# The second half of an out-projection by pairs of token tiles, with seven block products in place of eight for six of its eight k-tiles

## The chip, the cores and the metric

The kernel runs on one core of a Trainium2 chip. The time is device microseconds of one execution; a version is told by the median of its runs. PE is TensorE's matmul, PEld its weight load, DVE is VectorE, ACT is ScalarE, POOL is GpSimd and SP is SyncE, which issues nearly all DMA transfers. The chain of work, the durations and the waits come from a hardware trace of one profiled execution.

## The reference, cut to what matters

One layer: RMSNorm, an in-projection, a bidirectional state-space mixer with a gate, an out-projection with a residual add, and a final RMSNorm. There are 1024 tokens, `d_model` is 1024 and the mixer's inner width 2048. The change concerns the last four lines.

```python
u = rmsnorm(h, norm_w[i])
# ssd_mixer: in-projection, conv, scan in two directions, then
y = y.reshape(b, l, D_INNER) * jax.nn.silu(z.astype(jnp.float32))
yg = y.reshape(b, l, SSD_GROUPS, D_INNER // SSD_GROUPS)
yg = yg * lax.rsqrt(jnp.mean(yg * yg, axis=-1, keepdims=True) + EPS)
y = (yg.reshape(b, l, D_INNER) * norm_w.astype(jnp.float32)).astype(u.dtype)
out = y @ w_out                       # (1024, 2048) @ (2048, 1024)
h = h + out
return rmsnorm(h, final_norm_w)
```

## The kernel before

**Precision.** Each float32 operand of a large product is split into a high part (a cast to `fp32r`) and a low part (the rest, by a subtraction), and a product is three matmuls: high by high, high by low, low by high. In the names `yh` and `yl`, `wo..h` and `wo..l` are such pairs.

**Stages.** After RMSNorm, in-projection and convolution, eight groups of channels go through the scan (`ssd_units`), whose results `yt` are written to `y_d` in HBM, transposed. The out-projection takes the 2048 inner channels as 16 k-tiles of 128 rows, in two halves of 8. In the first half (`half` 0, weights `wo1`) `out_unit(0, t)` handles one tile of 128 tokens: 8 k-tiles by 3 passes by 2 column halves of 512, which is 48 matmuls into one accumulator `po` (128x1024 in PSUM). VectorE adds `po` to the residual `h` (line 565), and SyncE stores the sum in `h_d` (line 566). Units 0 to 3 stand between steps of the last scan group, units 4 to 7 behind it. The second half (`half` 1, weights `wo2`, loaded and scaled by `load_wo` two rows after each of the units 4 to 7) does the same from `h_d`, and then the final norm: add (line 571), square with a row sum on ScalarE (line 572), the root by `rstd_of` (lines 82 and 85), the scaling (lines 580 to 587) and the store to `out`. The last unit cuts its columns into 512, 256 and 256, in accumulators of their own, so that its adds and squares can begin early.

**Names.** In the profile and in the order, a name such as `h05` is the residual tile of half 0, token tile 5; `yt06` is the loaded slice of `y_d` for half 0, token tile 6, and `po10` the accumulator of half 1, tile 0.

**What sets the order.** `out_prep` issues the load of the next unit's `yt` (line 532) and `h` (line 534), and its cast (537) and subtraction (538), in the middle of a unit's matmuls. Every engine and the queue of SyncE work strictly in the order of the built program, and a DMA that must wait for a buffer or for a result holds what stands behind it in that queue. The order is fixed by a list scheduler when the program is built. Buffers are rooms of a pool, by tag: a new tile of a tag waits until the one that had its room is read. `yt` uses the tag `th` (2 rooms), the raw weight rows the tag `raw` (2 rooms), `h` the tag `xc` (3 rooms), `yh` and `yl` the tags `wh` and `wl` (4 rooms each).

Of the kernel before, what the change touches and what calls it, by code (L numbers as in the profile page):

```python
# [31 lines left out]
def kernel(  # L32
# [508 lines left out]
    def out_unit(half, t, wo, prep, nxt):  # L541
        h, yh, yl = prep
        tok = slice(t * P, (t + 1) * P)
        last = half == 1 and t == NC - 1
        cols = [slice(0, 512), slice(512, 1024)]
        ka = [(k, a) for k in range(NO) for a in range(3)]
        if last:

            cols[1:] = [slice(512, 768), slice(768, 1024)]
            steps = [(k, a, i) for i in range(3) for k, a in ka]  # L550
            pos = [pst(f"po{i}")[:, 0:cs.stop - cs.start] for i, cs in enumerate(cols)]
        else:
            po = ps_ip.tile([P, DM], F32, tag="ip", name=f"po{half}{t}")
            pos = [po[:, cs] for cs in cols]
            steps = [(k, a, i) for k, a in ka for i in range(2)]
        nprep = None
        for j, (k, a, i) in enumerate(steps):
            if j == len(steps) // 2 and nxt is not None:
                nprep = out_prep(*nxt)
            l_ = (yh, yh, yl)[a][:, k, :]  # L560
            r_ = wo[k][(0, 1, 0)[a]]
            nc.tensor.matmul(pos[i], l_, r_[:, cols[i]],  # L562
                             start=k == 0 and a == 0, stop=k == NO - 1 and a == 2)
        if half == 0:
            nc.vector.tensor_tensor(out=h, in0=po, in1=h, op=ALU.add)
            nc.sync.dma_start(out=h_d[tok, :], in_=h)
            return nprep
# [1 line left out]
        ss = ops.tile([P, 3], F32, tag="ss", name=f"oss{t}")
        for i, (cs, pi) in enumerate(parts):  # L570
            nc.vector.tensor_tensor(out=h[:, cs], in0=pi, in1=h[:, cs], op=ALU.add)  # L571
            nc.scalar.activation(out=pi, in_=h[:, cs], func=AF.Square, accum_out=ss[:, i:i + 1])
            if last:
                nc.vector.tensor_tensor(out=h[:, cs], in0=h[:, cs], in1=fnw[:, cs], op=ALU.mult)
# [75 lines left out]
```

## Time and profile before

| | before |
|---|---|
| median of 3 runs | 985.52 us (984.31 to 987.09) |
| the profiled execution's own time | 985.42 us |
| its span, first to last instruction | 983.7 us |
| PE busy | 945.5 us (96%), 5220 matmuls |
| VectorE busy | 727.9 us (74%) |
| ScalarE busy | 539.2 us (55%) |
| chain that ended last | PE 56%, VectorE 12%, DMA 12%, ScalarE 12% |

The span is that of the traced instructions; the execution's own time has 1.7 us around it. Busy shares are means over all stages. The chain that ended last is followed back from the last instruction, at each step to what released it; its shares say where a saved microsecond would show.

### The profile page before, as it was taken

What the parts mean: (1) busy time and instruction counts of PE and PEld (TensorE: products, weight loads), DVE (VectorE), ACT (ScalarE), POOL (GpSimd) and SP (SyncE); (2) the same over time, 40 slices, a digit from 0 to 9 for tenths busy, and PEclk for the clock granted to TensorE, in tenths of its full rate; (3) what the DMA queues carried; (4) which work ended last, traced back from release to release, by engine and by line L of the source; (5) the groups of instructions that cost most, each with busy time, mean ns of one, the idle gap of its engine ahead of it and who ended that gap; (6) DMA issues with size and microseconds to landing.
All of it is one profiled execution on the core that took longest, in us unless ns stands there. A gap on an engine that the chain in (4) does not pass through costs nothing.

```text
span 983.7 us, 15133 instructions
## 1 busy us (share of the span) xinstructions
PE 945.5 (96%) x5220; PEld 806.1 (82%) x5220; DVE 727.9 (74%) x1552; ACT 539.2 (55%) x1458; POOL 53.8 (5%) x88
## 2 busy tenths in 40 slices
...
GB/s 223 95 86 97 43 70 94 111 70 70 101 120 53 74 99 124 49 75 98 126 52 82 86 129 63 78 80 126 96 64 142 172 264 174 200 278 142 118 85 65
DMA packets 157325, 107.62 MB, mean 109 GB/s; under 512 B 75248, under 2 KB 133312, under 8 KB 157248
## 3 DMA queue, kind: packets, MB, share of 16 engines
...
## 4 chain that ended last, share of the span: by engine, by line
PE 56%; DVE 12%; DMA 12%; ACT 12%; issue 6%; POOL 2%; SPq 1%; DVEq 0%; POOLq 0%; ACTq 0%
PE po L562 16%; PE ipx L180 12%; PE ipC L180 9%; DMA fb<-rows_d 7%; PE ipB L180 7%; ACT yo L479 3%; DVE x L196 3%; ACT fb L424 2%; PE pz L157 2%; PE pyo L462 2%; PE pyd L468 2%; PE sb L393 2%; ACT fb L419 2%; DVE mt L429 1%; PE sf L393 1%
## 5 line engine op out<-in xcount | busy, mean ns | idle before, releaser
L479 ACT ACTIVATE yo<-pyo,ecs 128x64 f32<-128x64 f32 x448 | 103.1, 320 | 35.8 <-PE pyo L462 30.2
L419 ACT ACTIVATE fb<-fb,cfb 128x128 f32<-128x128 f32 x256 | 85.1, 399 | 55.1 <-DMA fb<-rows_d 49.6
L424 ACT ACTIVATE fb<-fb,cfb 128x128 f32<-128x128 f32 x256 | 84.0, 398 | 3.8 <-DVE fb L421 3.7
L196 DVE SCALAR_TENSOR_TENSOR x<-ipx,prm,x 128x1022 f32<-128x1022 f32 (+1 forms) x64 | 81.1, 1268 | 3.7 <-ACT x L190 3.6
L157 PE MATMUL pz<-wz_1l,uh 128*128 128x256 f32 (+1 forms) x248 | 73.0, 294 | 2.0 <-DVE wz_1l L123 2.0
L157 PE MATMUL pz<-wz_0h,ul 128*128 128x256 f32 (+1 forms) x248 | 73.3, 296 | 0.4 <-DVE ul L301 0.2
L157 PE MATMUL pz<-wz_0l,uh 128*128 128x256 f32 (+1 forms) x248 | 72.0, 290 | 0.0
L157 PE MATMUL pz<-wz_0h,uh 128*128 128x256 f32 (+1 forms) x248 | 71.2, 287 | 0.0
L157 PE MATMUL pz<-wz_1h,ul 128*128 128x256 f32 (+1 forms) x248 | 70.9, 286 | 0.0
L468 PEld LDWEIGHTS pyd<-xb,mt 128*128 128x128 f32 x512 | 66.7, 191 | 4.9 <-DVE mt L429 1.8
L157 PE MATMUL pz<-wz_1h,uh 128*128 128x256 f32 (+1 forms) x248 | 70.4, 284 | 0.0
L471 DVE SCALAR_TENSOR_TENSOR y<-xb,coef,pyd 128x64 f32<-128x64 f32 x256 | 62.5, 273 | 10.5 <-PE pyd L468 10.3
L468 PE MATMUL pyd<-xb,mt 128*128 128x64 f32 x512 | 64.7, 269 | 0.0
L429 DVE TENSOR_TENSOR mt<-fb,pcb 128x512 f32<-128x512 f32 x64 | 43.1, 681 | 15.3 <-PE pcb L427 13.0
L385 DVE TENSOR_TENSOR pb<-pb,sb 128x256 f32<-128x256 f32 x48 | 19.8, 412 | 42.0 <-PE sb L393 41.1
L421 DVE COPY_PREDICATED fb<-trif,fb 128x512 f32<-128x512 uint32 x64 | 47.1, 736 | 3.7 <-ACT fb L419 3.6
L157 PEld LDWEIGHTS pz<-wz_1l,uh 128*128 128x128 f32 x248 | 46.9, 189 | 3.4 <-DVE wz_1l L123 3.2
L157 PEld LDWEIGHTS pz<-wz_0h,ul 128*128 128x128 f32 x248 | 47.2, 190 | 1.3 <-DVE ul L301 1.1
L571 DVE TENSOR_TENSOR h<-po,h 128x1024 f32<-128x1024 f32 (+2 forms) x10 | 10.1, 1011 | 51.3 <-PE po L562 51.3
L157 PEld LDWEIGHTS pz<-wz_0h,uh 128*128 128x128 f32 x248 | 47.1, 190 | 0.5
L157 PEld LDWEIGHTS pz<-wz_0l,uh 128*128 128x128 f32 x248 | 47.1, 190 | 0.0
L157 PEld LDWEIGHTS pz<-wz_1h,ul 128*128 128x128 f32 x248 | 46.9, 189 | 0.2
...
## 6 DMA issues: line engine op xcount, KB each, us to landing
fb<-rows_d SPq DMA_DIRECT2D x128, 256.0 KB, 4.3
y_d<-yt SPq DMA_DIRECT2D x256, 32.0 KB, 2.0
wo<-in_ssd_w_out_dram SPq DMA_DIRECT2D x16, 512.0 KB, 4.2
yt<-y_d SPq DMA_DIRECT2D x16, 512.0 KB, 5.1
xt<-in_x_dram SPq DMA_DIRECT2D x8, 512.0 KB, 5.9
h<-in_x_dram SPq DMA_DIRECT2D x8, 512.0 KB, 4.8
h_d<-h SPq DMA_DIRECT2D x8, 512.0 KB, 3.0
h<-h_d SPq DMA_DIRECT2D x8, 512.0 KB, 3.6
```

Of the source, the lines that this page charges most:

```text
L157: nc.tensor.matmul(pz[:, i, 0:m], a[:, k, tok], b, start=at == 0, stop=at == 3 * NK - 1)
L180: nc.tensor.matmul(ps[:, half * 512:(half + 1) * 512], a[:, k, :], b[:, k, :], start=n == 0, stop=n == 3 * NK - 1)
L196: nc.vector.scalar_tensor_tensor(out=acc[:, o], in0=ps[:, i], scalar=w(k), in1=acc[:, o], op0=ALU.mult, op1=ALU.add)
L393: nc.tensor.matmul(ps[:, 0:CW], xb[:, CW:CW + P], xw, start=True, stop=True)
L419: nc.scalar.activation(out=ef[:, h], in_=ef[:, h], func=AF.Identity, bias=cfb[:, 1, c, hsl(g, h)])
L421: nc.vector.copy_predicated(ef, trif.bitcast(U32).unsqueeze(1).broadcast_to([P, HG, P]), fb[:, 0])
L424: nc.scalar.activation(out=ef[:, h], in_=ef[:, h], func=AF.Exp, bias=cfb[:, 0, c, hsl(g, h)])
L429: nc.vector.tensor_tensor(out=mt, in0=ef, in1=pcb[:, 0:P].unsqueeze(1).broadcast_to([P, HG, P]), op=ALU.mult)
L468: nc.tensor.matmul(pyd[:, cs], mt[:, h, :], xb[:, cs], start=True, stop=True)
L471: nc.vector.scalar_tensor_tensor(out=y[:, cs], in0=xb[:, cs], scalar=coef[:, h:h + 1], in1=pyd[:, cs], op0=ALU.mult, op1=ALU.add)
L479: nc.scalar.activation(out=yo[:, cs], in_=pyo[:, d * CW + h * HD:d * CW + (h + 1) * HD], func=AF.Copy, scale=ecs[:, d, c, hsl(g, h)])
L562: nc.tensor.matmul(pos[i], l_, r_[:, cols[i]], start=k == 0 and a == 0, stop=k == NO - 1 and a == 2)
```

## The change

The 2048 x 1024 product of the second half is rearranged for pairs of token tiles. For six of its eight k-tiles, taken as two groups of three (`HK`), two token tiles of a pair, the two groups and the two column halves make a 2 by 2 by 2 block product. It is computed with seven block products in place of eight, from sums and differences of the blocks:

- Weight operands: `w11`, `w21` (blocks themselves), `t1`, `t2`, `t3` (differences of blocks), made by `weights_a(k)` from two loaded and scaled rows, for k = 0, 1, 2 ahead of units 4, 5 and 6 of the first half; `w22` = `t2` + `t1` and `t4` = `w21` - `t2`, made on chip from the split parts of the others by `weights_b` behind unit 7.
- Token operands per pair: `a11`, `a12`, `a22` and `s1` to `s4`, made by `pair_prep` from two loaded `yt` tiles.
- The two k-tiles left over stay an ordinary product: weights `wd` (`weights_d`, ahead of unit 7) and token operand `e`, in four parts (`plain`) of 6 matmuls for a pair.

A block product is 9 matmuls (3 k-tiles by 3 passes) of 128 tokens by 512 columns. The results are shared among the four blocks of the output by accumulating in PSUM and by copies from one accumulator to another on ScalarE (lines 713, 721 and 732); one product (`pw`, named `p50` to `p53` in the program) is added to two blocks by VectorE (line 717). These line numbers are the changed kernel's. There `out_unit` has its matmuls in line 552, its add in 554 and its store in 555, `out_prep` loads in 533 and 535 and splits in 538 and 539; `split` casts in 589 and subtracts in 590, `scaled_row` loads in 594 and scales in 595; products are line 687, adds 696 with the square in 697. The five decay tables and `trif` move from the pool `const` to a pool `dec` that is closed after the scan.

```diff
--- before.py
+++ after.py
...
+    dec = main.enter_context(tc.tile_pool(name="dec", bufs=1))
+    cfb = dec.tile([P, 2, NC, NH], F32, name="cfb")
...
-        last = half == 1 and t == NC - 1
...
+        for k in range(NO):
...
+            for a in range(3):
+                for cs in (slice(0, 512), slice(512, 1024)):
+                    nc.tensor.matmul(po[:, cs], (yh, yh, yl)[a][:, k, :], wo[k][(0, 1, 0)[a]][:, cs],
+                                     start=k == 0 and a == 0, stop=k == NO - 1 and a == 2)
...
-        parts = list(zip(cols, pos)) if last else [(slice(0, DM), po)]
...
+        nc.vector.tensor_tensor(out=h, in0=po, in1=h, op=ALU.add)
+        nc.sync.dma_start(out=h_d[tok, :], in_=h)
...
+    HK = 3
+    LO, HI = slice(0, 512), slice(512, 1024)
+    def operand(pool, tag, name):
+        t_ = pool.tile([P, 2, HK, 512], R32, tag=tag, name=name)
+        return t_[:, 0], t_[:, 1]
+    def split(src, dst):
+        nc.scalar.copy(dst[0], src)
+        nc.vector.tensor_tensor(out=dst[1], in0=src, in1=dst[0].bitcast(F32), op=ALU.subtract)
+    def scaled_row(n):
+        raw = wp.tile([P, DM], F32, tag="raw", name=f"wa{n}", bufs=2)
+        nc.sync.dma_start(out=raw, in_=w_out[:, NO + n, :])
+        nc.scalar.activation(out=raw, in_=raw, func=AF.Copy,
+                             scale=prm[:, 192 + NO + n:193 + NO + n])
+        return raw
+    def minus(out, a, b):
+        nc.vector.tensor_tensor(out=out, in0=a, in1=b, op=ALU.subtract)
+    W = {n: operand(op2, "o" + n, "o" + n) for n in ("w11", "t1", "t2", "w21", "t3")}
+    wd = op2.tile([P, 2, 2, DM], R32, name="wd")
+    def weights_a(k):
+        ra, rb = scaled_row(k), scaled_row(k + HK)
+        r11, r12, r21, r22 = (r[:, cs] for r in (ra, rb) for cs in (LO, HI))
+        d3 = cp.tile([P, 512], F32, tag="th", name=f"da{k}")
+        split(r11, [p_[:, k] for p_ in W["w11"]])
+        minus(d3, r22, r12)
+        minus(r12, r12, r11)
+        split(r12, [p_[:, k] for p_ in W["t1"]])
+        minus(r22, r22, r12)
+        split(r22, [p_[:, k] for p_ in W["t2"]])
+        split(r21, [p_[:, k] for p_ in W["w21"]])
+        split(d3, [p_[:, k] for p_ in W["t3"]])
+    def weights_d():
+        for j in range(2):
+            split(scaled_row(2 * HK + j), [wd[:, p_, j] for p_ in range(2)])
+    def weights_b(n, a, b, op, tag):
+        W[n] = operand(up, tag, "o" + n)
+        for k in range(HK):
+            d = wp.tile([P, 2, 512], F32, tag="raw", name=f"d{n}{k}", bufs=2)
+            for p_ in range(2):
+                nc.vector.tensor_tensor(out=d[:, p_], in0=W[a][p_][:, k].bitcast(F32),
+                                        in1=W[b][p_][:, k].bitcast(F32), op=op)
+            nc.vector.tensor_tensor(out=d[:, 0], in0=d[:, 0], in1=d[:, 1], op=ALU.add)
+            split(d[:, 0], [p_[:, k] for p_ in W[n]])
+    def pair_prep(i):
+        ys, hs = [], []
+        for t in (2 * i, 2 * i + 1):
+            yt = cp.tile([P, NO, P], F32, tag="th", name=f"yt1{t}")
+            nc.sync.dma_start(out=yt, in_=y_v[:, NO:2 * NO, t * P:(t + 1) * P])
+            ys.append([yt[:, q].rearrange("p k t -> p (k t)")
+                       for q in (slice(0, HK), slice(HK, 2 * HK), slice(2 * HK, NO))])
+        for t in (2 * i, 2 * i + 1):
+            h = cp.tile([P, DM], F32, tag="xc", name=f"h1{t}", bufs=3)
+            nc.sync.dma_start(out=h, in_=h_d[t * P:(t + 1) * P, :])
+            hs.append(h)
+        (a11, a12, e1), (a21, a22, e2) = ys
+        A = {}
+        rooms = {}
+        N = HK * P
+        def put(n, *srcs):
+            at = len(A)
+            if at % 2 == 0:
+                rooms["h"] = wp.tile([P, 2, 512], R32, tag="wh", name=f"yh{i}_{n}", bufs=4)
+                rooms["l"] = wp.tile([P, 2, 512], R32, tag="wl", name=f"yl{i}_{n}", bufs=4)
+            m = len(srcs) * srcs[0].shape[1]
+            room = [rooms[p_][:, at % 2, 0:m] for p_ in "hl"]
+            for j, src in enumerate(srcs):
+                c = slice(j * m // len(srcs), (j + 1) * m // len(srcs))
+                split(src, [r[:, c] for r in room])
+            A[n] = [r.rearrange("p (k t) -> p k t", t=P) for r in room]
+        def room(n):
+            t_ = wp.tile([P, 2, 512], F32, tag="raw", name=f"s{n}_{i}", bufs=2)
+            return t_[:, 0, 0:N], t_[:, 1, 0:N]
+        put("a11", a11)
+        s1, s2 = room("a")
+        nc.vector.tensor_tensor(out=s1, in0=a21, in1=a22, op=ALU.add)
+        put("s1", s1)
+        minus(s2, s1, a11)
+        put("s2", s2)
+        put("a12", a12)
+        put("e", e1, e2)
+        s3, s4 = room("b")
+        minus(s3, a11, a21)
+        put("s3", s3)
+        minus(s4, a12, s2)
+        put("s4", s4)
+        put("a22", a22)
+        return A, hs
+    def product(ps, a, w, fresh, cs=LO, end=True):
+        n, last = 0, 3 * a[0].shape[1] - 1
+        for k in range(a[0].shape[1]):
+            for l_, r_ in ((a[0], w[0]), (a[0], w[1]), (a[1], w[0])):
+                nc.tensor.matmul(ps, l_[:, k, :], r_[:, k, cs], start=fresh and n == 0,
+                                 stop=end and n == last, skip_group_check=True)
+                n += 1
+    def plain(ps, A, j, cs, end):
+        product(ps, [p_[:, 2 * j:2 * j + 2] for p_ in A["e"]], (wd[:, 0], wd[:, 1]), False, cs, end)
+    def add(h, cs, ps, ss, i):
+        nc.vector.tensor_tensor(out=h[:, cs], in0=ps, in1=h[:, cs], op=ALU.add)
+        nc.scalar.activation(out=ps, in_=h[:, cs], func=AF.Square, accum_out=ss[:, i:i + 1])
+        if i:
+            nc.vector.tensor_tensor(out=ss[:, 0:1], in0=ss[:, 0:1], in1=ss[:, i:i + 1], op=ALU.add)
+    def finish(t, h, ss):
+        r = rstd_of(ops, ss[:, 0:1], DM, EPS, f"o{t}")
+        nc.vector.scalar_tensor_tensor(out=h, in0=h, scalar=r, in1=fnw, op0=ALU.mult, op1=ALU.mult)
+        nc.sync.dma_start(out=out[t * P:(t + 1) * P, :], in_=h)
+    def pair_unit(i, prep, nxt):
+        A, (h1, h2) = prep
+        t1, t2 = 2 * i, 2 * i + 1
+        ss1, ss2 = (ops.tile([P, 3], F32, tag="ss", name=f"oss{i}_{j}") for j in range(2))
+        c1 = ps_ip.tile([P, DM], F32, tag="ip", name=f"po1{i}")
+        c11, c12 = c1[:, LO], c1[:, HI]
+        product(c12, A["a11"], W["w11"], True)
+        nc.scalar.copy(c11, c12)
+        pw = pst(f"p5{i}")
+        product(pw, A["s1"], W["t1"], True)
+        for h in (h1, h2):
+            nc.vector.tensor_tensor(out=h[:, HI], in0=pw, in1=h[:, HI], op=ALU.add)
+        product(c12, A["s2"], W["t2"], False)
+        c2 = ps_ip.tile([P, DM], F32, tag="ip", name=f"po2{i}")
+        c21, c22 = c2[:, LO], c2[:, HI]
+        nc.scalar.copy(c22, c12)
+        product(c11, A["a12"], W["w21"], False, end=False)
+        plain(c11, A, 0, LO, True)
+        nprep = pair_prep(nxt) if nxt is not None else None
+        add(h1, LO, c11, ss1, 0)
+        if nxt is None:
+            plain(c12, A, 0, HI, False)
+            product(c12, A["s4"], W["w22"], False)
+            add(h1, HI, c12, ss1, 1)
+            finish(t1, h1, ss1)
+        product(c22, A["s3"], W["t3"], False)
+        nc.scalar.copy(c21, c22)
+        plain(c22, A, 1, HI, True)
+        add(h2, HI, c22, ss2, 0)
+        if nxt is not None:
+            plain(c12, A, 0, HI, False)
+            plain(c21, A, 1, LO, False)
+            product(c12, A["s4"], W["w22"], False)
+            add(h1, HI, c12, ss1, 1)
+            product(c21, A["a22"], W["t4"], False)
+            finish(t1, h1, ss1)
+            add(h2, LO, c21, ss2, 1)
+            finish(t2, h2, ss2)
+            return nprep
+        nc.vector.tensor_tensor(out=h2[:, HI], in0=h2[:, HI], in1=fnw[:, HI], op=ALU.mult)
+        for j, cs in enumerate((slice(0, 256), slice(256, 512))):
+            plain(c21[:, cs], A, 1, cs, False)
+            product(c21[:, cs], A["a22"], W["t4"], False, cs)
+        for j, cs in enumerate((slice(0, 256), slice(256, 512))):
+            add(h2, cs, c21[:, cs], ss2, 1 + j)
+            nc.vector.tensor_tensor(out=h2[:, cs], in0=h2[:, cs], in1=fnw[:, cs], op=ALU.mult)
...
     fnw = op2.tile([P, DM], F32, name="fnw")
+    for t in range(NC // 2, NC):
+        if t < NC - 1:
+            weights_a(t - NC // 2)
+        else:
+            weights_d()
+            pre0 = pair_prep(0)
+        prep = out_unit(0, t, wo1, prep, (0, t + 1) if t < NC - 1 else None)
     nc.sync.dma_start(out=fnw, in_=final_norm_w.rearrange("(o d) -> o d", o=1).partition_broadcast(P))
-    wo2 = []
...
-    for t in range(NC):
-        prep = out_unit(1, t, wo2, prep, (1, t + 1) if t < NC - 1 else None)
+    weights_b("w22", "t2", "t1", ALU.add, "uh0")
+    weights_b("t4", "w21", "t2", ALU.subtract, "ul0")
+    prep = pre0
+    for i in range(NC // 2):
+        prep = pair_unit(i, prep, i + 1 if i + 1 < NC // 2 else None)
```

The order of the built program is shown at three places. The first is the queue of SyncE around the store of `h05`, in the first half's unit 5. Before, the loads of `yt06` and `yt07` stand here:

```order
L532 DMA yt06_9348<-y_d_81 128x8x128
L496 DMA y_d_81<-yt7_5_9083 32x8x32 x4
L566 DMA h_d_8163<-h03_8925 128x1024
L532 DMA yt07_9415<-y_d_81 128x8x128
L532 DMA yt10_9484<-y_d_81 128x8x128
L496 DMA y_d_81<-yt7_6_9208 32x8x32 x4
L534 DMA h06_9350<-in_x_dram 128x1024
L532 DMA yt11_9551<-y_d_81 128x8x128
L566 DMA h_d_8163<-h04_9116 128x1024
L496 DMA y_d_81<-yt7_7_9240 32x8x32 x4
L534 DMA h07_9417<-in_x_dram 128x1024
L532 DMA yt12_9617<-y_d_81 128x8x128
```

The store of `h05` follows behind these. In the changed program its surroundings are these, where `wa1` to `wa7` are rows of weights, and `h10`, `yt10` and `yt11` belong to pair 0:

```order
L594 DMA wa1_9342<-in_ssd_w_out_dram 128x1024
L594 DMA wa4_9345<-in_ssd_w_out_dram 128x1024
L555 DMA h_d_8166<-h05_9310 128x1024
L533 DMA yt06_9387<-y_d_76 128x8x128
L644 DMA h10_9514<-h_d_8166 128x1024
L594 DMA wa2_9421<-in_ssd_w_out_dram 128x1024
L594 DMA wa5_9424<-in_ssd_w_out_dram 128x1024
L533 DMA yt07_9466<-y_d_76 128x8x128
L639 DMA yt10_9510<-y_d_76 128x8x128
L594 DMA wa6_9500<-in_ssd_w_out_dram 128x1024
L594 DMA wa7_9505<-in_ssd_w_out_dram 128x1024
L639 DMA yt11_9512<-y_d_76 128x8x128
```

The loads of `yt06` and `yt07` have moved behind the store of `h05`, and they have loads of weights around them.

The second place is VectorE behind the same add of `h05`. Before:

```order
L565 TENSOR_TENSOR h05_9281<-po05_9323,h05_9281 128x1024
L538 TENSOR_TENSOR yl11_9556<-yt11_9551,yh11_9555 128x1024
L521 SCALAR_TENSOR_TENSOR wo1l0_9314<-wo12_9382,prm_74,wo1h0_9313 128x1024
L521 SCALAR_TENSOR_TENSOR wo1l0_9314<-wo13_9386,prm_74,wo1h0_9313 128x1024
L565 TENSOR_TENSOR h06_9350<-po06_9390,h06_9350 128x1024
L521 SCALAR_TENSOR_TENSOR wo1l1_9450<-wo14_9451,prm_74,wo1h1_9449 128x1024
```

In the changed program, with the operands of weights named `ow11` to `ow21` and `ot1` to `ot4`:

```order
L554 TENSOR_TENSOR h05_9310<-po05_9362,h05_9310 128x1024
L590 TENSOR_TENSOR ow11_9256<-wa1_9342,ow11_9256 128x512
L600 TENSOR_TENSOR da1_9348<-wa4_9345,wa1_9342 128x512
L590 TENSOR_TENSOR ow21_9259<-wa4_9345,ow21_9259 128x512
L600 TENSOR_TENSOR wa1_9342<-wa1_9342 128x512
L590 TENSOR_TENSOR ot3_9260<-da1_9348,ot3_9260 128x512
L600 TENSOR_TENSOR wa4_9345<-wa4_9345,wa1_9342 128x512
L590 TENSOR_TENSOR ot1_9257<-wa1_9342,ot1_9257 128x512
L590 TENSOR_TENSOR ot2_9258<-wa4_9345,ot2_9258 128x512
L539 TENSOR_TENSOR yl06_9392<-yt06_9387,yh06_9391 128x1024
L590 TENSOR_TENSOR ow11_9256<-wa2_9421,ow11_9256 128x512
L600 TENSOR_TENSOR da2_9427<-wa5_9424,wa2_9421 128x512
```

Between two adds of the first half stood three instructions, all of 1024 columns; now the operand work of `weights_a` stands there, in instructions of 512 columns, and the subtraction for `yl06` has eight of them ahead of it. Some 45 rows further on in the changed program the work of `weights_b` (lines 629, 631 and 590, with `dw22k` and `dt4k` as its raw rows) stands directly ahead of the operands of pair 1:

```order
L631 TENSOR_TENSOR dw222_9615<-dw222_9615 128x512
L629 TENSOR_TENSOR dt40_9622<-ow21_9259,ot2_9258 128x512 x2
L590 TENSOR_TENSOR ow22_9602<-dw222_9615,ow22_9602 128x512
L631 TENSOR_TENSOR dt40_9622<-dt40_9622 128x512
L629 TENSOR_TENSOR dt41_9628<-ow21_9259,ot2_9258 128x512 x2
L590 TENSOR_TENSOR ot4_9621<-dt40_9622,ot4_9621 128x512
L631 TENSOR_TENSOR dt41_9628<-dt41_9628 128x512
L629 TENSOR_TENSOR dt42_9634<-ow21_9259,ot2_9258 128x512 x2
L590 TENSOR_TENSOR ot4_9621<-dt41_9628,ot4_9621 128x512
L631 TENSOR_TENSOR dt42_9634<-dt42_9634 128x512
L717 TENSOR_TENSOR h11_9516<-p50_9653,h11_9516 128x512
L590 TENSOR_TENSOR yl1_a11_9700<-yt12_9691,yh1_a11_9699 128x384
```

The third place is TensorE in pair 0, at the point where operands of pair 1 are first used. A name of a room stands for two operands there: `yh0_e` also holds `s3`, and the second half of `yh1_a11` holds `s1`. Waits are those for semaphores of other engines:

```order
L687 MATMUL po20_9674<-ot3_9260,yh0_e_9533 128x512 x2
L687 MATMUL po20_9674<-ot3_9260,yl0_e_9534 128x512
L687 MATMUL po20_9674<-wd_9261,yh0_e_9533 128x512 [waits Activation_49]
L687 MATMUL po20_9674<-wd_9261,yh0_e_9533 128x512
L687 MATMUL po20_9674<-wd_9261,yl0_e_9534 128x512
L687 MATMUL po20_9674<-wd_9261,yh0_e_9533 128x512 x2
L687 MATMUL po20_9674<-wd_9261,yl0_e_9534 128x512
L687 MATMUL p51_9812<-ot1_9257,yh1_a11_9699 128x512 [waits Activation_49]
L687 MATMUL p51_9812<-ot1_9257,yh1_a11_9699 128x512
L687 MATMUL p51_9812<-ot1_9257,yl1_a11_9700 128x512 [waits DVE_49]
L687 MATMUL p51_9812<-ot1_9257,yh1_a11_9699 128x512 x2
```

The product `p51` of pair 1 has been taken forward into pair 0, behind a product, a copy and a plain part, and it waits for ScalarE and then for VectorE. On ScalarE the copies between the accumulators stand among the casts of operands:

```order
L713 COPY po10_9642<-po10_9642 128x512 [waits PE_49]
L589 CAST yh1_a11_9699<-yt12_9691 128x384 [waits DMAHW1_49,PE_49,Activation_49]
L589 CAST ow22_9602<-dw221_9609 128x512 [waits DVE_49]
L721 COPY po20_9674<-po10_9642 128x512 [waits PE_49,Activation_49]
L589 CAST ow22_9602<-dw222_9615 128x512 [waits DVE_49]
L589 CAST yh1_s2_9708<-yt12_9691 128x384 [waits PE_49]
L589 CAST ot4_9621<-dt40_9622 128x512 [waits DVE_49]
L732 COPY po20_9674<-po20_9674 128x512 [waits PE_49]
```

The copy of line 721 is queued behind the cast for `ow22`, which waits for VectorE.

## Rows read from the trace of the kernel before

**Rows 1.** Chain of work that ended last, 840 to 984 us: start, us, what

```profile
844.72 132.46 PE po L562 x591
```

**Rows 2.** Stretches: length, busy PE, PEld, DVE, ACT, POOL, clock, DMA share, GB/s

```profile
860.00:888.00 28.00, 28.00 (x121) 22.52 (x120) 14.96 (x13) 11.40 (x11) 0.00 (x0) 1.00 0.84 274
888.00:977.00 89.00, 89.00 (x406) 72.64 (x404) 27.46 (x32) 13.65 (x23) 3.84 (x7) 1.00 0.30 101
...
982.00:983.70 1.70, 0.00 (x0) 0.00 (x0) 0.00 (x0) 0.00 (x0) 0.00 (x0) 0.61 0.20 74
```

**Rows 3.** Matmuls of L562, second half: ns min/median/max, first and last start, forms

```profile
L562 PE MATMUL po<-wo1h,yh x136: 274/392/398, 887.3 to 976.6; 128*128 128x512 f32 x120, 128*128 128x256 f32 x16
```

**Rows 4.** Timeline of PE: start, us, operation; idle before and releaser in brackets

```profile
864.91 0.63 PE L562 MATMUL po<-wo0h,yh 128*128 128x512 f32 x2
...
887.31 0.62 PE L562 MATMUL po<-wo1h,yh 128*128 128x512 f32 x2
887.78 0.63 PE L562 MATMUL po<-wo1l,yh 128*128 128x512 f32 x2
```

**Rows 5.** Timeline of DVE around 865 us

```profile
865.11 1.23 DVE L565 TENSOR_TENSOR h<-po,h 128x1024 f32<-128x1024 f32 x1 [2.06 <-PE po L562]
866.25 1.22 DVE L538 TENSOR_TENSOR yl<-yt,yh 128x1024 fp32r<-128x1024 f32 x1
```

**Rows 6.** Timeline of SyncE's queue (SPq): start and length of issues

```profile
836.47 1.80 SPq L496 DMA_DIRECT2D y_d<-yt  x4
840.67 3.74 SPq L532 DMA_DIRECT2D yt<-y_d  x2
...
866.37 0.33 SPq L566 DMA_DIRECT2D h_d<-h  x1
```

**Rows 7.** Transfers issued from 850 us on: count, KB each, us to landing

```profile
h<-h_d SPq DMA_DIRECT2D x8, 512.0 KB, 3.6
yt<-y_d SPq DMA_DIRECT2D x7, 512.0 KB, 4.2
wo<-in_ssd_w_out_dram SPq DMA_DIRECT2D x6, 512.0 KB, 5.3
fnw<-in_final_norm_w_dram SPq DMA_DIRECT2D x1, 512.0 KB, 6.2
```

**Rows 8.** Groups of DVE by shape: count, busy us, mean ns, idle before

```profile
L301 DVE TENSOR_TENSOR ul<-pu,uh 128x512 fp32r<-128x512 f32 x16 | 10.1, 678 | 0.0
```

**Rows 9.** Groups of ACT by shape; the last row from 850 us on

```profile
L300 ACT CAST uh<-pu 128x512 fp32r<-128x512 f32 x16 | 8.6, 596 | 1.7 <-PE pu L295 1.7
...
L520 ACT ACTIVATE wo1h<-wo,prm 128x1024 fp32r<-128x1024 f32 x8 | 9.1, 1150 | 17.4 <-DMA wo<-in_ssd_w_out_dram 12.4 <-DMA y_d<-yt 4.9
...
L537 ACT CAST yh<-yt 128x1024 fp32r<-128x1024 f32 x9 | 9.4, 1049 | 42.4 <-PE po L562 24.7 <-issue 16.7 <-DMA yt<-y_d 0.7
```

**Rows 10.** Timeline of DVE at the end

```profile
968.41 0.15 DVE L82 TENSOR_SCALAR o6m<-oss 128x1 f32<-128x1 f32 x1 [1.28 <-ACT po L572]
969.29 1.28 DVE L586 SCALAR_TENSOR_TENSOR h<-h,o6r,fnw 128x1024 f32<-128x1024 f32 x1 [0.73 <-POOL o6r L85]
...
971.51 0.69 DVE L571 TENSOR_TENSOR h<-po,h 128x512 f32<-128x512 f32 x1 [0.93 <-PE po L562]
972.99 0.69 DVE L574 TENSOR_TENSOR h<-h,fnw 128x512 f32<-128x512 f32 x1 [0.79 <-ACT po L572]
...
977.20 0.42 DVE L571 TENSOR_TENSOR h<-po,h 128x256 f32<-128x256 f32 x1 [1.35 <-PE po L562]
978.20 0.42 DVE L574 TENSOR_TENSOR h<-h,fnw 128x256 f32<-128x256 f32 x1 [0.58 <-ACT po L572]
```

**Rows 11.** Timeline of PE at the start

```profile
7.96 1.97 PE L295 MATMUL pu<-ident,u 128*128 128x128 f32 x8 [7.96 <-DVE u L290]
...
15.94 0.47 PE L157 MATMUL pz<-wz_1h,uh 128*128 128x320 f32 x1
16.59 0.31 PE L157 MATMUL pz<-wz_1h,uh 128*128 128x320 f32 x1
```

More of the change, by code (lines that the diff above doesn't have):

```diff
@@ L91 @@
     main = ExitStack()
+    dec = main.enter_context(tc.tile_pool(name="dec", bufs=1))
+    cfb = dec.tile([P, 2, NC, NH], F32, name="cfb")
+    ecs = dec.tile([P, 2, NC, NH], F32, name="ecs")
+    wdt = dec.tile([P, 2, NC, NH], F32, name="wdt")
+    dcy = dec.tile([P, 2, NC, NH], F32, name="dcy")
+    dtb = dec.tile([P, NC, NH], F32, name="dtb")
     bp = main.enter_context(tc.tile_pool(name="bp", bufs=2))
@@ L543, in out_unit @@
         tok = slice(t * P, (t + 1) * P)
-        last = half == 1 and t == NC - 1
[L545 to L555, printed above, removed]
+        po = ps_ip.tile([P, DM], F32, tag="ip", name=f"po{half}{t}")
@@ L556, in out_unit @@
         nprep = None
-        for j, (k, a, i) in enumerate(steps):
-            if j == len(steps) // 2 and nxt is not None:
+        for k in range(NO):
+            if k == NO // 2 and nxt is not None:
                 nprep = out_prep(*nxt)
[L560 to L567, printed above, removed]
@@ L568, in out_unit @@
-        parts = list(zip(cols, pos)) if last else [(slice(0, DM), po)]
[L569 to L574, printed above, removed]
-            if i:
-                nc.vector.tensor_tensor(out=ss[:, 0:1], in0=ss[:, 0:1], in1=ss[:, i:i + 1],
-                                        op=ALU.add)
```

31 lines of the change are left out of this document (6 added, 25 removed).

## Prediction

> **What bounds the kernel now.** I read the chain of work that ended last first: from 844.72 us on it is one entry, 132.46 us of L562, the matmuls of the out-projection, and it ends 6.5 us before the span does [rows 1]. So in this stage a matmul that goes saves its whole time, as long as TensorE finds its operands ready. The busy times by stretch say how much room the others have: from 860 to 888 us VectorE works 14.96 of 28 us and ScalarE 11.40, and from 888 to 977 us 27.46 and 13.65 of 89 [rows 2]. That looks like ample room, but the change does not spread its work evenly, and what decides is when each operand is ready.
>
> **Sizes.** The second half has 136 matmuls of each of its three kinds, 120 of 512 columns and 16 of 256 (one kind is shown) [rows 3]: in all 384 of 512 columns, counting two halves as one. Two of them start 0.47 us apart from the next two, so one costs 0.2335 us, and a unit of 48 is 11.2 us: two units lie between 864.91 and 887.31 [rows 4]. TensorE goes from one unit to the next without a gap. Adds of `po` to `h` start 0.2 us after the next unit has begun (865.11 against 864.91) [rows 4, 5].
>
> **What the change removes.** A pair of token tiles takes 7 products of 9 matmuls and 4 plain parts of 6, which is 87 in place of 96; four pairs save 36 matmuls, 36 x 0.2335 = **-8.4 us**.
>
> **What it adds ahead of the pairs.** I follow the order of the changed program from the add of `h05` at 865.11 (call it T0), where unit 5 of the first half has ended.
>
> *The load for unit 6.* Before, SyncE had the loads of `yt06` and `yt07` out long ahead (issued from 840.67) [rows 6]. Now `yt06` stands behind the store of `h05`, and that store waits for the add. It is issued at T0 + 1.26 as it is now, an issue takes 0.45 (four in 1.80) [rows 6], so `yt06` leaves at T0 + 1.7, needs 4.2 to land [rows 7] and a cast of 1.05 [rows 9]: T0 + 7.0. ScalarE is free by then: its casts for `ot1` and `ot2` wait on six VectorE instructions of 512 columns after the add and end at T0 + 5.4. TensorE restarts at 872.1 instead of 864.91, a wait of **7.2 us**, and 0.3 more for the low half.
>
> *VectorE's backlog.* A 512-column subtraction takes 0.678 [rows 8], and one starts 0.08 before its predecessor ends (1.23 against 866.25 - 865.11 = 1.14) [rows 5], so each costs 0.60; by the same line 384 columns cost 0.47, 256 cost 0.33, 1024 cost 1.14. From T0 to the low half of `s1` of pair 1 the order has 67 instructions: 42 of 512, 16 of 384, 2 of 256, 7 of 1024, together 41.2 us of pure work. TensorE without any wait would be at the product that needs this operand (`p51`, taken forward behind the first 57 matmuls of pair 0) at T0 - 0.2 + 22.4 + 57 x 0.2335 = T0 + 35.5. So VectorE is at least 5.7 us late even if no transfer holds it. But transfers do. The eighth instruction frees `wa2`'s room at T0 + 5.4; its load lands 5.3 later [rows 7], ScalarE scales, casts, scales (1.15, 0.6, 1.15, slightly overlapped) [rows 9] to T0 + 13.4; four VectorE steps give the room of `yt10` free at T0 + 15.9; this load lands at 20.1 and is cast by T0 + 20.7. From here 48 instructions remain, 28.2 us. One more wait lies in them: `wd` needs `wa6`, whose load leaves at T0 + 17.1, lands 5.3 later and is scaled and cast at T0 + 24.6, where VectorE has been free since 22.8: 1.8. The operand is ready at T0 + 50.7, or **915.8 us**.
>
> *TensorE's way there.* 872.1 + 0.3 + 22.4 for units 6 and 7 + 13.3 for 57 matmuls = 908.1 (unit 7 starts at T0 + 18.5, and its `yh07` is cast by T0 + 18.2, behind the same VectorE steps). Three copies between accumulators lie on it. Such a copy reads what TensorE has just finished, and the next product waits for it: 0.16 until the last matmul ends (0.39 long, the next may start after 0.23), 0.6 for 512 columns out of PSUM (the nearest row is a cast of that size) [rows 9], two hand-overs of 0.03: 0.8. The first is mostly covered by the product for `p50` (0.45 remains), the third costs 0.8; the second stands in ScalarE's queue behind a cast of `ow22` that waits for VectorE, 2.3. That gives 911.7; two matmuls of `p51` (0.5) need no low half, so TensorE waits another 3.6 us for VectorE. Since VectorE's chain hangs on T0 and not on TensorE, a shorter wait at unit 6 would only lengthen this one.
>
> **From 915.8 to the end.** 289 matmuls remain, 67.5 us. Waits on the way: in pair 0 the square of `h10` before the accumulator opens again, three more VectorE instructions, an add and a square (1.41 + 1.48 by the 512-column add at 971.51 and its follower at 972.99 [rows 10]) against 1.63 of matmuls, 1.2. In pairs 1 to 3 seven copies or squares stand directly between two products, 7 x 0.8 = 5.6. In the last pair `plain` on `c21` waits for add and square of the other half of `h17`, behind the whole finish of `h16`: 0.19 + 1.48 + 0.1 + 0.88 (968.41 to 969.29) + 1.20 + 1.48 [rows 10] = 5.3 against 2.4 of TensorE's own, so 2.9. Sum 9.7; the last matmul ends at 993.0 against 977.2 [rows 1], about +16.0 with its last 0.16.
>
> *The tail.* Both 256-column pieces now stand in one bank, and both adds come after all matmuls. One more add, square and product lie behind the end: 978.20 - 977.20 + 0.35 = **+1.35** [rows 10].
>
> **The sum.** 16.0 + 1.35 = +17.4, which is -8.4 for the products and +25.8 of waits: 7.5 at unit 6, 3.6 (copies) and 3.6 (VectorE) in pair 0 up to `p51`, 9.7 behind it, 1.35 in the tail. The profiled execution took 985.42, with a span of 983.7, and the median is 985.52, so they agree. **985.5 + 17.4, about 1003 us.** Bounds of the unknown terms: landings of 3.6 or 6.2 us, the quickest and slowest load of this stretch [rows 7], for those of 4.2 and 5.3 move the chain to 915.8 by -3 to +4; a copy may cost 0.6 (nothing but itself) or 1.2 (if it ran like a cast of 1024 columns, 1.05, with hand-overs) [rows 9], over ten places -2 to +4. The scaled rows of `wa0` and `wa3`, which ScalarE now does inside the scan's last groups, I cost at nothing: TensorE's matmuls of units 3 and 4 cover them; without that cover it is 2 x 1.15 [rows 9].
>
> **The clock.** A gap of 7 us is longer than any that this trace has between its first and last matmul, so its price must be bounded. In the first stretch TensorE, from 7.96 us, ran at its lower level: a matmul of 320 columns took 0.47 at 15.94 and 0.31 at 16.59 [rows 11]. After the last matmul the granted clock has fallen within the stretch from 982 us, to a mean of 0.61 [rows 2]. If it falls in the gap and stays as long as in the first stretch, 8.4 us, half of it is lost, 4.2. But the chain to 915.8 runs on VectorE and SyncE, and TensorE has 3.6 us to spare there: I take 0 and keep 0 to 2 for this gap and up to 4.2 for one at `p51`. The Trainium skill, TensorE: Matmul & The Clock Gate, Part 1, states that the default is the throttled 1.2 GHz, and that activity releases it and idleness brings it back. By that rule the clock falls at unit 6 for certain. The rows at the start and the end agree; what it costs here no run has shown yet.
>
> **The rivals.**
> - *All operands are in time.* Then only matmuls go: 985.5 - 8.4 + 1.35 = 978.4. It holds from the point where all waits together stay under 7.0 us. Against it stand 41.2 us of VectorE work for 35.5 us, and ten copies with nothing between. Chance 4% (0.03 faster, 0.01 about even).
> - *VectorE keeps nearly up.* Loads land early and ScalarE's queue does not hold VectorE. With the wait at unit 6 as above `p51` then starts when TensorE comes, 3.6 earlier, 999; with an early `yt06` too it waits for the pure work alone, T0 + 41.2 in place of 50.7: 1003 - 9.5 = 993.5. Copies and tail stay. 13%.
> - *The clock falls twice, or loads are late.* The gap at `p51` also drops the clock (+4.2), or loads take 6.2 us (+4): 1007 to 1012. 23%.
> - *My sum*, 999 to 1007: 60%.
> That the matmuls would not go is no case: the order of the changed program has 9 and 6 where I count them.
>
> **How the numbers follow.** The likeliest is 1003. From 996 to 1012 leaves out most of the 4%, less than half of the 13% and a little above. A change under 0.3%, 3 us, is about what a measurement of this kernel can't tell from none; nearly everything here lies beyond it: faster 0.03, same 0.01, slower 0.96.
>
> **What would show it.** In the profile after, matmuls of L687 and L552 drop by 36 x 512 columns and TensorE has a gap of 7 us ahead of unit 6, released by ScalarE's cast of `yh06`, that by the load of `yt06`. VectorE is busy without a break for some 25 us ahead of `p51`, and TensorE waits there about 4 us. Every pair shows gaps of 0.8 behind L713, L721 or L732, the last one of 3 us behind L697. I am wrong if `yt06` lands before unit 5 ends, if VectorE is idle ahead of `p51`, or if the accumulator copies cost TensorE nothing.

## The result and the profile after

The changed kernel takes **1008.36 us** (median of 4 runs, 1007.66 to 1009.55) against 986.31 (4 runs, 984.31 to 988.40): ratio **1.023**, interval 1.0217 to 1.0243, about 22 us slower. The forecast was 1003, with a range of 996 to 1012. The profiled execution took 1009.55 with a span of 1007.8. It has 5175 matmuls, 45 fewer than before: the 36 of 512 columns that were to go, and 9 because the last pair is cut otherwise.

The busy times of the changed kernel by stretch, in the columns of [rows 2]:

```profile
866.00:888.00 22.00, 14.45 (x50) 11.15 (x50) 12.96 (x19) 12.59 (x16) 0.00 (x0) 0.77 0.55 169
888.00:920.00 32.00, 26.96 (x114) 20.67 (x112) 28.35 (x47) 14.24 (x24) 0.00 (x0) 1.00 0.50 154
920.00:960.00 40.00, 35.75 (x146) 26.85 (x147) 24.48 (x48) 15.85 (x38) 2.20 (x4) 1.00 0.40 122
960.00:1000.00 40.00, 35.48 (x162) 27.59 (x160) 17.73 (x34) 10.75 (x26) 1.65 (x3) 1.00 0.25 89
```

Before the change TensorE was busy without a break from 860 to 977 us [rows 2]. Now it works 14.45 of 22 us, 26.96 of 32, 35.75 of 40 and 35.48 of 40, and the first of the four has a mean granted clock of 0.77. What TensorE waited for from 868 us on, by line: total, times and the longest.

```profile
PE po L552 <- ACT yh L538: 7.5, 1, 7.5
PE po L687 <- ACT po L697: 4.3, 4, 2.8
PE po L687 <- ACT po L721: 4.1, 4, 2.0
PE p L687 <- ACT yh_a L589: 3.0, 1, 3.0
PE po L687 <- ACT po L732: 1.3, 2, 0.7
PE po L687 <- ACT po L713: 0.9, 1, 0.9
```

All waits end with ScalarE, which says nothing yet about who is late: its casts, copies and squares are the last step of every chain. 7.5 us stand ahead of unit 6, 3.0 ahead of `p51`, and 10.6 in eleven stops at copies (L713, L721, L732) and squares (L697). The chain of unit 6 in the timelines, SyncE first, then VectorE, ScalarE and TensorE:

```profile
861.45 0.91 SPq L594 DMA_DIRECT2D wa<-in_ssd_w_out_dram  x2
...
869.37 0.33 SPq L555 DMA_DIRECT2D h_d<-h  x1
869.74 0.43 SPq L533 DMA_DIRECT2D yt<-y_d  x1
...
873.58 1.11 SPq L594 DMA_DIRECT2D wa<-in_ssd_w_out_dram  x2
...
885.32 0.38 SPq L639 DMA_DIRECT2D yt<-y_d  x1
886.53 1.12 SPq L594 DMA_DIRECT2D wa<-in_ssd_w_out_dram  x2
```

```profile
868.12 1.23 DVE L554 TENSOR_TENSOR h<-po,h 128x1024 f32<-128x1024 f32 x1 [6.70 <-PE po L552]
...
881.69 0.69 DVE L590 TENSOR_TENSOR ow<-wa,ow 128x512 fp32r<-128x512 f32 x1 [4.86 <-ACT ow L589]
...
894.41 1.23 DVE L590 TENSOR_TENSOR wd<-wa,wd 128x1024 fp32r<-128x1024 f32 x1 [2.11 <-ACT wd L589]
```

```profile
874.53 1.04 ACT L538 CAST yh<-yt 128x1024 fp32r<-128x1024 f32 x1 [0.93 <-DMA yt<-y_d]
...
879.86 1.15 ACT L595 ACTIVATE wa<-wa,prm 128x1024 f32<-128x1024 f32 x1 [4.29 <-DMA wa<-in_ssd_w_out_dram]
```

```profile
875.63 1.22 PE L552 MATMUL po<-wo0h,yh 128*128 128x512 f32 x2 [7.55 <-ACT yh L538]
876.65 1.05 PE L552 MATMUL po<-wo0l,yh 128*128 128x512 f32 x2
...
882.27 0.63 PE L552 MATMUL po<-wo0h,yl 128*128 128x512 f32 x2
...
909.41 0.73 PE L687 MATMUL po<-ow,yh_s 128*128 128x512 f32 x2 [1.96 <-ACT po L721]
...
920.58 0.73 PE L687 MATMUL p<-ot,yh_a 128*128 128x512 f32 x2 [3.00 <-ACT yh_a L589]
921.44 0.50 PE L687 MATMUL p<-ot,yl_a 128*128 128x512 f32 x1
...
996.06 0.50 PE L687 MATMUL po<-wd,yh_e 128*128 128x256 f32 x2 [2.84 <-ACT po L697]
```

The add of `h05` starts at 868.12, its store follows at 869.37 and the load of `yt06` at 869.74; the cast that needs this load starts at 874.53, and TensorE restarts at 875.63, 7.51 us behind the add. The weight rows leave in pairs, at 861.45, 873.58 and 886.53, 12 to 13 us apart: each pair waits for its two rooms until VectorE has finished with the pair before. VectorE stands idle for 4.86 us before it has the next rows, and for 2.11 before `wd`.

The matmul rows show two things that recur. After the gap two matmuls together take 1.05 in place of 0.63; the granted clock there is 0.50, the lower of its two levels (the rows stand further below). And after the stops at full clock the first two take 0.73, not 0.63: a stop costs about 0.1 us more than the idle time in brackets says, besides the 0.16 that the last matmul ahead of it runs on.

### The profile page after: what moved, and what is told of

It reads as the page before. It is cut to its first block, busy times and chain, and to the rows that moved or that the text cites. A ratio compares the mean times of both kernels' runs of the same rounds, so it can differ in the third digit from the quotient of the medians.

```text
span 1007.8 us, 15251 instructions
## 1 busy us (share of the span) xinstructions
PE 943.9 (94%) x5175; PEld 798.9 (79%) x5175; DVE 771.8 (77%) x1660; ACT 569.7 (57%) x1535; POOL 54.3 (5%) x88
## 5 line engine op out<-in xcount | busy, mean ns | idle before, releaser
L472 DVE SCALAR_TENSOR_TENSOR y<-xb,coef,pyd 128x64 f32<-128x64 f32 x256 | 62.5, 273 | 10.6 <-PE pyd L469 10.1
L386 DVE TENSOR_TENSOR pb<-pb,sb 128x256 f32<-128x256 f32 x48 | 19.8, 413 | 42.0 <-PE sb L394 41.2
L552 PE MATMUL po<-wo0h,yh 128*128 128x512 f32 x128 | 43.1, 416 | 7.5 <-ACT yh L538 7.5
```

The costliest lines, as they stand in the source:

```text
L386: nc.vector.tensor_tensor(out=st, in0=st, in1=ps[:, 0:CW], op=ALU.add)
L472: nc.vector.scalar_tensor_tensor(out=y[:, cs], in0=xb[:, cs], scalar=coef[:, h:h + 1], in1=pyd[:, cs], op0=ALU.mult, op1=ALU.add)
L552: nc.tensor.matmul(po[:, cs], (yh, yh, yl)[a][:, k, :], wo[k][(0, 1, 0)[a]][:, cs], start=k == 0 and a == 0, stop=k == NO - 1 and a == 2)
```

## The experiments

Ratios are against the kernel before, measured on the same chip. Its median was 982.9 beside `own_banks`, `early_yt06`, `more_rooms` and `rooms_and_banks`, 982.7 on another chip beside `changed_again`, `no_weights_b`, `tail_two_banks` and `copies_covered`, and 986.3 beside the first result.

**Unit 5 ended 3 us later: is that the change?** The add of `h05` stands at 868.12, while it was at 865.11 before [rows 5]. Two further profiles, `changed_again` and `before_again`, are of the same two kernels, each on another chip:

> The changed kernel once more, so that it stands on the same chip as the runs beside it. Ratio to before 1.022 to 1.024. If the 3 us by which unit 5 of the first half ended later in its first profile belong to that execution or chip, its end comes within 1 us of that of the other kernels of this call; if they belong to the change, 3 us later than before's 865.1 again, and later than in the kernels with other rooms.

> The kernel before once more, for the time at which unit 5 of the first half ends. If that moves from execution to execution by some us whatever the kernel, it lies between 860 and 864 us here, as in the changed kernels on this chip, and not at 865.1 as in the first profile; the stretch from there to the last matmul is again 111.8 us. If the change delays that point, it lies 2 us or more under the 862.3 of the changed kernel.

`changed_again` took 1004.32 us (1002.90 to 1006.59), ratio 1.0215 (1.0196 to 1.0234); its profiled execution is the longest of the four. `before_again`, one execution, took 982.74. The add of `h05` in `changed_again`, then in `before_again`:

```profile
862.29 1.23 DVE L554 TENSOR_TENSOR h<-po,h 128x1024 f32<-128x1024 f32 x1 [6.71 <-PE po L552]
```

```profile
862.43 1.22 DVE L565 TENSOR_TENSOR h<-po,h 128x1024 f32<-128x1024 f32 x1 [2.06 <-PE po L562]
```

They differ by 0.14 us. Between the two profiles of one kernel the point moves by 2.7 us before and by 5.8 after the change, so the 3 us do not show a delay. The loss lies behind the add: from there to the end of the span it is 118.6 us in both profiles of before (983.7 - 865.1, 981.0 - 862.4), and 139.7 and 142.6 in those of the changed kernel, 21.1 and 24.0 more. Between the medians it is 22.1 and 21.7.

**own_banks: no tile shared between two column halves.** In the changed kernel `c11` and `c12` are halves of one tile, and so are `c21` and `c22`. Each half has a PSUM bank, but a wait is set for the tile. Here each becomes a tile of one bank; `bank` takes it from a pool of four that replaces `ps_ip`.

```diff
-        c1 = ps_ip.tile([P, DM], F32, tag="ip", name=f"po1{i}")
-        c11, c12 = c1[:, LO], c1[:, HI]
+        c11, c12 = bank(f"c11_{i}"), pst(f"c12_{i}")
...
-        c2 = ps_ip.tile([P, DM], F32, tag="ip", name=f"po2{i}")
-        c21, c22 = c2[:, LO], c2[:, HI]
+        c22 = bank(f"c22_{i}")
...
+        c21 = bank(f"c21_{i}")
```

> Each accumulator of a pair (c11, c12, pw, c22, c21) is a tile and a PSUM bank of its own; nothing else is changed. Theory of the prediction (a product that stands behind a copy needs its data, so the stop is real): only the last pair's 2.9 us and some of the squares go, 1003 to 1007 us. Rival (the stops behind line 721 and line 697 are waits for a tile as a whole, because the two column halves share one): seven stops of 0.7 to 1 us and the 2.8 us of the last pair go, and with them the two or three us that ScalarE's queue adds in pair 0: 993 to 999 us. The gap of 7.5 us ahead of unit 6 stays in both.

987.62 us (985.83 to 989.39), ratio 1.0038 (1.0024 to 1.0051), below both expectations. TensorE's waits from 860 us on:

```profile
PE po L553 <- ACT yh L539: 7.4, 1, 7.4
PE c L688 <- ACT c L732: 1.5, 4, 0.7
```

All waits for L721, L697 and L713 are gone; only L732 is left, where the next matmul really writes what the copy reads. TensorE behind the same copy as L721, in pair 0:

```profile
901.82 0.39 PE L688 MATMUL c<-ot,yl_s 128*128 128x512 f32 x1
902.05 0.62 PE L688 MATMUL c<-ow,yh_s 128*128 128x512 f32 x2
```

The two products follow one another as in the changed kernel, without its stop of 1.96 us. In the last pair `plain` on `c21` likewise starts (976.00) before the square of `c22` does (976.92), where the changed kernel has its stop of 2.84. So the product behind L721, which writes `c11`, had waited for a copy that reads `c12`; `plain` on `c21` in the last pair had waited for the square of the other half. The order elsewhere also changed: `p51` went back into its own pair and did not wait for VectorE any more. How much of the 17 us each of the two is worth, this run does not separate.

The Trainium skill, Perfetto Trace Analysis, Optimizing Tensor Performance (Matmuls), asks that independent groups of matmuls rotate through different banks, so that emptying one overlaps the next. The trace agrees: nothing is left of the 4.1 us of waits at L721. It adds that different banks were not enough while the program saw one tile.

**early_yt06: the load of unit 6 in time, the weight rows as they were.**

```diff
-        d3 = cp.tile([P, 512], F32, tag="th", name=f"da{k}")
+        d3 = op2.tile([P, 512], F32, tag="da", name=f"da{k}")
```

(`dbc` moves from `const` to `dec` to make the space.)

> The difference operand da of weights_a gets a room of its own, so that the loads of yt06 to yt11 stand ahead of the store of h05 as they did before the change; the weight rows still go through two raw rooms. Theory of the prediction (the chain of weights to pair 0 and p51 hangs on the end of unit 5 and sets the time; a shorter wait at unit 6 lengthens a later one): no gap ahead of unit 6, a gap of 7 to 13 us at the first products of pair 0 instead, 1003 to 1016 us. Rival (the late yt06 is the cause of the loss): 7.5 us of gap and some 3 us of slow clock go, 997 to 999 us.

1006.04 us (1005.44 to 1006.94), ratio 1.0233 (1.0219 to 1.0247): no gain at all. TensorE's wait for operands in `p50` and `p51`, the issues of weight rows, and TensorE, VectorE and clock by stretch:

```profile
PE p L687 <- ACT yh_a L589: 14.9, 2, 8.5
```

```profile
859.09 3.64 SPq L594 DMA_DIRECT2D wa<-in_ssd_w_out_dram  x2
...
871.03 1.49 SPq L594 DMA_DIRECT2D wa<-in_ssd_w_out_dram  x2
...
882.20 1.11 SPq L594 DMA_DIRECT2D wa<-in_ssd_w_out_dram  x2
```

```profile
894.00:898.00 4.00, 3.96 (x9) 2.98 (x10) 4.00 (x10) 2.37 (x6) 0.00 (x0) 0.50 0.15 40
...
912.00:918.00 6.00, 2.43 (x6) 1.78 (x7) 6.00 (x13) 1.64 (x3) 0.00 (x0) 0.50 0.00 0
```

The gap ahead of unit 6 is gone, and two others have come, 8.5 us at `p50` and 6.4 at `p51`: 14.9 in place of 7.5 + 3.0. The weight rows still leave 11 to 12 us apart, and TensorE works at a granted clock of 0.50 behind each of the two gaps.

**more_rooms: the weight rows in rooms that stood idle.** The arithmetic is the same.

```diff
-        raw = wp.tile([P, DM], F32, tag="raw", name=f"wa{n}", bufs=2)
+        raw = wp.tile([P, DM], F32, tag=tag, name=f"wa{n}", bufs=4)
...
-        ra, rb = scaled_row(k), scaled_row(k + HK)
+        ra, rb = scaled_row(k, "wh"), scaled_row(k + HK, "wl")
...
-        d3 = cp.tile([P, 512], F32, tag="th", name=f"da{k}")
+        d3 = wp.tile([P, 512], F32, tag="raw", name=f"da{k}", bufs=2)
```

> The weight rows of weights_a and weights_d are loaded into rooms of the tags wh and wl (4 each) in place of the two raw rooms, and da into a raw room; the arithmetic and the number of instructions are the same. If the two raw rooms (12.5 us for load, scaling and splitting of two rows, one after the other) set the time up to p51: no gap at unit 6, no clock fall, under 1 us of wait at p51, 992 to 996 us. If VectorE's work itself sets it (41 us of instructions from the end of unit 5 on): still 4 to 6 us at p51, 998 to 1001 us.

990.76 us (989.48 to 994.57), ratio 1.0083 (1.0063 to 1.0104), a little below the lower of the two expectations. The stretch behind unit 5 and some of TensorE's waits:

```profile
863.00:888.00 25.00, 25.00 (x109) 20.12 (x108) 22.79 (x35) 12.95 (x22) 0.00 (x0) 1.00 0.62 203
```

```profile
PE po L687 <- ACT po L697: 3.8, 2, 2.9
PE po L687 <- ACT po L721: 2.9, 4, 0.7
...
PE p L687 <- ACT yh_a L589: 0.6, 1, 0.6
```

TensorE is busy without a break to 888, and 0.6 us are left at `p51`. VectorE has as many instructions as in the changed kernel, but works 22.79 of the 25 us behind unit 5, where in the changed kernel it works 15.88 of the 26 from 868 to 894. So its work fits, once it can begin. It also begins earlier: nine of the 67 instructions that the prediction counted from the add of `h05` to `p51` now stand ahead of that add, and 58 are left behind it. Nine of the eleven stops in the pairs are still there.

**no_weights_b: less work for VectorE, the rooms as they were.** The kernel leaves out `weights_b` and takes `t1` and `t2` for its two operands, so that it computes something else.

```diff
-    weights_b("w22", "t2", "t1", ALU.add, "uh0")
-    weights_b("t4", "w21", "t2", ALU.subtract, "ul0")
+    W["w22"], W["t4"] = W["t1"], W["t2"]
```

> weights_b is left out: w22 and t4 are set to the finished operands t1 and t2, so two products per pair are taken with other weights; 24 subtractions, additions and low parts of 512 columns on VectorE and 6 casts on ScalarE go, all of them between the operands of pair 0 and those of pair 1. If VectorE's work behind the last weight rows sets the start of p51 (20 us without a break up to it): no wait at p51 and 0.9 in place of 2.1 us at the copy of line 721 in pair 0, 5 us saved, with p51 in its own pair another 2: 6 to 9 us under the changed kernel. If only the turnaround of the raw rooms counts: under 2 us. The gap of 7.6 us ahead of unit 6 stays.

995.97 us (994.32 to 997.43), ratio 1.0134 (1.0116 to 1.0152), 8.35 us under `changed_again`, as expected of VectorE's work. Two of the waits:

```profile
PE po L552 <- ACT yh L538: 7.5, 1, 7.5
PE po L687 <- ACT po L721: 2.8, 4, 0.7
```

No wait at `p51` is left, and the longest at L721 is 0.7 in place of 2.0; `p51` is also back in its own pair, which is part of the gain. Behind the last weight rows VectorE's work did set the time, since it began late; ahead of them the rooms did, and the 7.5 us at unit 6 stay.

**rooms_and_banks, tail_two_banks, copies_covered: the versions that beat both.** The first has the edits of `own_banks` and `more_rooms`. The second copies `c21` of the last pair into two banks, 256 columns in each. The third also puts work between the copy to `c21` and the plain part that overwrites `c22`: the plain part of `c12`, in the last pair all that is left of `c12`'s work. Of the second and the third edit:

```diff
+            c2s = [bank(f"c21_{i}{j}")[:, 0:256] for j in range(2)]
+            for j in range(2):
+                nc.scalar.copy(c2s[j], c22[:, j * 256:(j + 1) * 256])
...
+        if nxt is not None:
+            plain(c12, A, 0, HI, False)
         plain(c22, A, 1, HI, True)
```

> Both of own_banks and more_rooms. If the two losses are separate and add up, next to nothing but the 36 saved matmuls, one stop per pair at most and the longer tail is left: 978 to 983 us, faster than before the change. If VectorE's work is the bound behind them: 986 to 992 us.

> rooms_and_banks, and in the last pair c21 is copied into two banks, 256 columns each, so that the add and square of the first 256 can run beside the products of the second. Prediction's term: 1.35 us of the tail come back, 0.9935 of before where rooms_and_banks had 0.9949. Rival (the second copy stands in the way of the first product, or the first add is not on the chain): within 0.4 us of rooms_and_banks.

> tail_two_banks, and the plain part of c12 stands between the copy to c21 and the plain part of c22, in the last pair the whole of c12's work. What is left of stops between products in rooms_and_banks (0.7 and 0.9 us and some of 0.1 to 0.2) is the true wait for a copy: 1 to 2 us less than tail_two_banks, 0.992 of before, 977 us where before is 985. Rival (other work in the way, or the finish of h16 now comes later and delays the end): no change.

| | median us | ratio to before | interval |
|---|---|---|---|
| rooms_and_banks | 977.66 | 0.9949 | 0.9936 to 0.9962 |
| tail_two_banks | 976.99 | 0.9939 | 0.9926 to 0.9953 |
| copies_covered | 975.51 | 0.9924 | 0.9909 to 0.9939 |

All three are faster than before the change, by 0.5 to 0.8%, with whole intervals under 1. Of TensorE's waits only those at the copy to `c21` are left in them, 0.3 to 1.2 us in all. Between neighbours the intervals overlap, so the steps of the second and third are read from the trace. From the add that waits for the last matmul to the scaling with the root it is 3.81 us in `rooms_and_banks`, where a second add still follows, and 2.29 in `tail_two_banks`, 1.5 less:

```profile
968.03 0.42 DVE L697 TENSOR_TENSOR h<-c,h 128x256 f32<-128x256 f32 x1 [1.40 <-PE c L688]
...
971.84 0.49 DVE L754 TENSOR_SCALAR h<-h,o7r 128x512 f32<-128x512 f32 x1 [0.73 <-POOL o7r L81]
```

```profile
967.40 0.42 DVE L697 TENSOR_TENSOR h<-c,h 128x256 f32<-128x256 f32 x1 [0.28 <-PE c L688]
...
969.69 0.49 DVE L759 TENSOR_SCALAR h<-h,o7r 128x512 f32<-128x512 f32 x1 [0.73 <-POOL o7r L81]
```

In `copies_covered`, TensorE's only line of waits from unit 6 on, and most of the stretch up to the last matmul:

```profile
PE c L688 <- ACT c L728: 0.3, 1, 0.3
```

```profile
888.00:965.00 77.00, 76.38 (x342) 61.65 (x340) 51.29 (x97) 30.55 (x72) 4.09 (x7) 1.00 0.35 112
```

0.3 us of waits are left. Of the 8.4 us that the 36 matmuls are worth, 7.5 are gained (985 x 0.0076).

## Why the prediction was right, and what was off

The direction, the place and most of the sizes held. The sum came out somewhat larger: from the end of unit 5 it is 139.7 - 118.6 = 21.1 us in the first profile, where +17.4 had been forecast. With 1008 us the time lies not within the prediction's sum (999 to 1007) but where it had put the rival of a second fall of the clock or late loads (1007 to 1012, 23%); the repeat, 1.0215, would be 1006.7 at 985.5. The first profile does not show that rival either: the clock fell once and cost nothing, and the loads came up to 1.0 us late. The 3.7 us are small excesses in several terms. The stretch of low clock in the gap, the two from the end of unit 5 to `p51`, and the add behind the last matmul:

```profile
872.00:880.00 8.00, 4.37 (x10) 3.47 (x11) 3.47 (x5) 2.20 (x4) 0.00 (x0) 0.50 0.89 269
```

```profile
868.00:894.00 26.00, 18.45 (x68) 14.64 (x68) 15.88 (x22) 13.62 (x19) 0.00 (x0) 0.80 0.69 208
894.00:921.00 27.00, 21.38 (x90) 16.16 (x88) 26.43 (x45) 12.05 (x23) 0.00 (x0) 1.00 0.36 111
```

```profile
999.93 0.42 DVE L696 TENSOR_TENSOR h<-po,h 128x256 f32<-128x256 f32 x1 [3.20 <-PE po L687]
```

- *The matmuls go.* 45 fewer, and with the waits removed in `copies_covered` nearly their whole price came back.
- *Unit 6.* 7.2 forecast, 7.55 measured, by the chain of store, load and cast that was named. One reading was off without harm: the two loads at 840.67 [rows 6] are those of `yt07` and `yt10`; `yt06` had left at 834.65.
- *A shorter wait at unit 6 would only lengthen the next.* `early_yt06` showed it: ratio 1.0233 against 1.023.
- *The operand of `p51`.* T0 + 50.7 forecast; the first matmul with the low half starts at 921.44, T0 + 53.3. This term, +2.6, is the largest error. The load of `wa2` took 6.3 (issued 873.58, scaled from 879.86) for the 5.3 of [rows 7], and `yt10` leaves at T0 + 17.2 for T0 + 15.9, 1.3 late. VectorE waits 2.11 for `wd` where 1.8 were reckoned, and the last 1.0 is spread over the 48 instructions behind. VectorE then works 26.43 of the 27 us up to `p51`; 25 had been forecast.
- *The clock.* It fell in the gap, to 0.50 from 872 to 880. TensorE worked some 6 us at half speed, about 3 lost; since it still waited 3.00 at `p51`, that cost nothing in this execution, as reckoned. The Trainium skill, TensorE: Matmul & The Clock Gate, Part 1, cited in the prediction, has it that idleness brings the throttle back; the trace agrees. In `changed_again` the clock fell twice more, around the stop of 1.96 us at L721 and behind the wait of 2.87 at `p51`. The second of these is the rival's case; from the operand to the end of the matmuls it took 80.4 us there, 1.9 more than in the first profile:

```profile
903.00:906.00 3.00, 2.93 (x8) 2.34 (x9) 3.00 (x6) 0.64 (x2) 0.00 (x0) 0.60 0.36 146
917.00:920.00 3.00, 2.94 (x9) 1.80 (x8) 2.76 (x5) 1.34 (x4) 0.00 (x0) 0.54 0.00 0
```

- *From the operand to the last matmul.* 77.4 forecast (67.5 + 9.7, and 0.16 in which the last matmul ends), 999.93 - 921.44 = 78.5 measured. A stop between two products cost about 0.97 (0.71 idle, 0.16 of the last matmul, 0.1 at the restart), not 0.8; the one in the last pair is 2.84 idle for 2.9.
- *The tail.* +1.35 forecast; 1007.8 - 999.93 against 983.7 - 977.20 [rows 10] is +1.4.

Two causes were told wrongly or in part, though their sizes held. "Such a copy reads what TensorE has just finished, and the next product waits for it" describes L713 and L732. At L721 and L697, which held 8.4 of the 10.6 us, the product needed nothing from the copy or the square: `own_banks` took those waits away. The size came out because the wait for the tile ends with the same copy. And the lateness at `p51` was put down to 41.2 us of VectorE's work for 35.5 us of time, with transfers on top. The count is right for this order, 67 instructions; but `more_rooms` shows that the order hangs on the rooms. Two raw rooms for eight rows held the work back, and with more of them part of it was done ahead of the add and 0.6 us of wait were left. So the case "all operands are in time", with 4%, was not out of reach for a lack of VectorE time: `rooms_and_banks` reached 0.9949, which is 980.5 at 985.5, where the rival had 978.4.
